# First column block of a decoder trunk: earlier shift and scale, low halves on two engines, earlier row scaling, filler products

## The chip, the core and the metric

The kernel runs on one core of a Trainium2 chip. A core has a matrix engine (TensorE, in the profile PE, its weight loads PEld), a vector engine (VectorE, DVE), an engine for activation functions (ScalarE, ACT), a general one (GpSimd, POOL) and a queue that issues transfers (SyncE, SP). Each runs its own instructions in order and waits for the others by semaphores. The metric is the device time of one execution in microseconds (us); less is better.

## What is computed

One layer of a hybrid decoder on a sequence of 2048 positions by 1024 channels, in float32. The part that matters here is its beginning:

```python
c_act = jax.nn.silu(c)
mod = c_act @ w_ada + b_ada
sh1, sc1, gt1, sh2, sc2, gt2 = jnp.split(mod, 6, axis=-1)
h = rms_norm(x, g_mix) * (1.0 + sc1) + sh1
p = h @ w_in            # columns for attention, mLSTM and spatial gating
...
x = x + gt1 * (y @ w_out)
h = rms_norm(x, g_ffn) * (1.0 + sc2) + sh2
x = x + gt2 * conv_ffn(h)
```

A shift and a scale of 1024 values each come from a vector times a matrix; every row of x is divided by its root mean square; scale and shift are applied by channel; then h goes through the input projection.

## The kernel before

**Arithmetic.** Products are exact to about float32 by splitting each operand into a rounded high half and the low half that is left (`hh` and `hl` of the activations, `wh` and `wl` of the weights). One product of two tiles is three matmuls: high by high, high by low, low by high (`mm3`, lines 54 to 56).

**Shift and scale.** `w_ada` is read in tiles of 128 rows by 512 columns, eight tiles (k = 0 to 7) for each group of 512 columns. Groups 0 and 1 give the shift, groups 2 and 3 the scale; 0 and 2 belong to channels 0 to 511, the first column block, 1 and 3 to channels 512 to 1023, the second. Tile 0 of a group goes to TensorE by itself (`column_sum(n, ada[n][0], cs)`): four products with a moving operand of one column, which the profile shows as eight instructions. Tiles 1 to 7 are multiplied by their column of `cs` and added up on DVE (`part`, lines 1116 and 1118), and the sum goes to TensorE as one more column sum (`column_sum(n, macc[n], ones)`). `first_columns` (lines 501 to 503) turns the sums of one column block into `sh1` and `a1`, with three small DVE instructions.

**First block.** Everything around the change is in `first_block` (lines 1082 to 1273). Its order is written out by hand: inside `tc.manual_schedule()` each engine runs its instructions exactly as the program lists them, through the first six of the fourteen steps of the input projection; most of what comes later is ordered by a planner. The block handles rows 0 to 511 (`x0`, four tiles of 128 rows) and then rows 512 to 1023 (`x1`, four tiles). For each tile of rows: squares with a sum on ACT (`squares`), the moments (`moments`: two small DVE instructions and a power on POOL at line 128), and a scaling by that root (`scale0` on ACT for `x0`, `scale` on DVE at line 1127 for `x1`). TensorE transposes the tiles (`turn_part`, line 611) into eight column tiles k = 0 to 7, each 128 channels by 512 rows.

`make_part(tb, k, ps)` takes one transposed tile from PSUM: ACT applies scale and shift (line 602), the high half is made on DVE or, with `on_scalar`, on ACT (line 603), and the low half on DVE (line 606). The argument `between` lets `part` steps of the next column block run on DVE between the high and the low half. `prod(t, tt, k)` multiplies 128 rows of that tile by the weights of the first projection block, 272 columns wide: three matmuls. `cur.cast()` makes the halves of those weights, the high one on ACT (line 647), the low one on POOL (line 648). The 16 gate columns of the weights are copied in by POOL (line 1159).

So the order was: sums of the first column block; eight weight casts; `part(1, 1)`; `first_columns(0)`; tiles k = 0 to 3 of the first 512 rows, with the `part(1, k)` steps between; their products; then sums of the second column block; the squares of two tiles of `x1`; `first_columns(1)`; tiles 4 to 7 and their products; the other squares; scaling of all of `x1` on DVE; its transpositions; `finish(0)`, which copies the results out and adds the gate biases (lines 1226 and 1227); and the same products for the second 512 rows.

**Loads** are all issued on SP's queue in program order: `x0`, the first and third group of `w_ada`, the block's weights, the second and fourth group, the three gate biases (lines 1091 to 1093, each spread to 128 partitions), `x1`, the weights of the next block (`nx`), small rows.

Of the kernel before, what the change touches and what calls it, by code (L numbers as in the profile page):

```python
# [8 lines left out]
F32 = mybir.dt.float32  # L9
# [8 lines left out]
P = 128  # L18
# [15 lines left out]
def trunk(  # L34
# [443 lines left out]
    def load_rest():  # L478
        r = pool.tile([P, P], F32, name="rows", tag="kw")
        dma(r[0:8], g_ffn[0].rearrange("(k p) -> k p", p=P))  # L480
        for i, g in enumerate((g_q, g_k)):
            for j in range(2):
                dma(r[8 + i : 9 + i, 64 * j : 64 * j + 64], g)
        dma(r[10:14], b_s[0])
        dma(r[14:16], g_m_out[0].rearrange("(k p) -> k p", p=P))
        return r
# [82 lines left out]

    def squares(parts):  # L570
        st = pool.tile([P, 2], F32, name="st", tag="st")
        for q, t in enumerate(parts):
            jk = pool.tile([P, 512], F32, name="jk", tag="sq")
            A.activation(jk, t, AF.Square, accum_out=st[:, q : q + 1])
        return st

    def moments(st):
        V.tensor_tensor(st[:, 0:1], st[:, 0:1], st[:, 1:2], op=ALU.add)
        V.tensor_scalar(st[:, 0:1], st[:, 0:1], 1.0 / D, EPS, op0=ALU.mult, op1=ALU.add)
        rsqrt(st[:, 0:1], 1)  # L580

    def halves(xt):
        return xt[:, 0:512], xt[:, 512:1024]
# [13 lines left out]

    def make_part(tb, k, ps, on_scalar=False, between=()):
        h32 = pool.tile([P, TB], F32, name="h32", tag="t2k")
        hh = pool.tile([P, TB], F32R, name="hh", tag="hT")  # L600
        hl = pool.tile([P, TB], F32R, name="hl", tag="hT")
        A.activation(h32, ps, AF.Identity, bias=sh1[:, k : k + 1], scale=a1[:, k : k + 1])
        (A.copy if on_scalar else V.tensor_copy)(hh, h32)
        for f in between:
            f()
        V.tensor_tensor(hl, h32, hh.bitcast(F32), op=ALU.subtract)  # L606
        hT[tb, k] = (hh, hl)

    def turn_part(ps, xs, k, i):
# [472 lines left out]
    def first_block():  # L1082
# [6 lines left out]
        for n in (1, 3):  # L1089
            ada[n] = list(load_ada(n * 512, "hT"))  # L1090
        dma(gbias[:, 0:8], b_fox_f.broadcast_to([P, 8]))
        dma(gbias[:, 8:12], b_m_i.broadcast_to([P, 4]))
        dma(gbias[:, 12:16], b_m_f.broadcast_to([P, 4]))
        x1 = []
# [11 lines left out]
        for k in range(KT):  # L1106
            nx.load()
        r16 = load_rest()
        dma(gsgu, g_sgu.broadcast_to([P, 256]))
# [15 lines left out]

        def scale(x, st):
            V.tensor_scalar(x, x, st[:, 0:1], None, op0=ALU.mult)

        def scale0(i):
            A.activation(x0[i], x0[i], AF.Copy, scale=st[i][:, 0:1])  # L1130
            turns0(i)

        st = [squares(halves(t)) for t in x0[:2]]
        moments(st[0])
        moments(st[1])
        scale0(0)
        st.append(squares(halves(x0[2])))
# [15 lines left out]
        column_sum(0, macc[0], ones[:, 0:1])  # L1153
        for k in range(4, 8):
            part(2, k)
        column_sum(2, macc[2], ones[:, 0:1])

        for k in range(KT):
            G.tensor_copy(cur.raw[k][:, 256:272], gw[:, k, :])
        for _ in range(KT):  # L1160
            cur.cast()
        part(1, 1)
        first_columns(0)
        ps = [pp.tile([P, 512], F32, name="acc", tag="acc2"), mps()]
# [11 lines left out]

        pair = lambda k: [lambda k=k: part(1, k), lambda k=k: part(1, k + 1)]
        make_part(0, 0, tp[0], True, pair(2))
# [4 lines left out]
        make_part(0, 1, tp[1], True, pair(4))  # L1183
        prod(0, 0, 1)
        prod(0, 1, 1)
        make_part(0, 2, tp[2], True, pair(6))
        tp.append(turns(x0, 5))
        prod(0, 0, 2)
        prod(0, 1, 2)
        make_part(0, 3, tp[3], True)  # L1190
        prod(0, 0, 3)
        prod(0, 1, 3)
        n_acc[0] += 1
# [5 lines left out]
        column_sum(1, macc[1], ones[:, 0:1])  # L1199
        for k in range(1, 8):  # L1200
            part(3, k)
        column_sum(3, macc[3], ones[:, 0:1])
        st = [squares(t) for t in x1[:2]]
        for t in st:
            moments(t)
        first_columns(1)
        for k in (4, 5):
            make_part(0, k, tp[k])
            tp.append(turns(x0, k + 2))
        st.append(squares(x1[2]))  # L1210
        moments(st[2])
        for tt in range(4):
            prod(0, tt, 4)
        for k in (6, 7):
            make_part(0, k, tp[k])
            for tt in range(4):
                prod(0, tt, k - 1)
        for tt in range(4):
            prod(0, tt, 7)
        st.append(squares(x1[3]))  # L1220
        moments(st[3])

        def finish(t0):
# [8 lines left out]

        for i in range(4):
            for t in x1[i]:
                scale(t, st[i])
        tps = [tr_ps(), tr_ps()]
        for i in range(4):
            for k in range(2):
                turn_part(tps[k], x1, k, i)
        finish(0)  # L1240
# [836 lines left out]
```

## Time and profile before

| | us |
|---|---|
| median of 3 runs | 2570.06 |
| lowest, highest | 2568.8, 2570.49 |
| span of the profiled execution, first to last instruction | 2567.7 |
| share of the span in which PE is busy | 98% |
| first group's products of column tiles 0 to 3 | 31.39 to 40.22 |
| shift and scale of the second column block taken up on DVE | 42.99 |
| first group's products of column tiles 4 to 7 | 46.27 to 54.07 |
| second group's first product | 56.33 |

The profile records one execution. Its page shows the span; the runs' median is 2.4 us above it, the rest lying before the first and after the last instruction. A line of a timeline gives the start, the time taken, the engine, the line of the kernel, the operation, the tile written and the tiles read with their shapes, how many instructions were merged, and in brackets how long the engine had been idle and what it was waiting for. In a view of groups the numbers after the bar are the busy time, the mean of one instruction in ns, and the idle time ahead. The granted clock of TensorE is 1.00 at full speed. Matmul ends in the trace are modelled and overlap the next start, so the step from one start to the next is what a matmul costs.

### The profile page before, as it was taken

Reading aid. Unit: us, or ns where it says so; the run is one execution under the profiler, and the core shown is the slowest. Engines: PE = TensorE matmul, PEld = TensorE weight load, DVE = VectorE, ACT = ScalarE, POOL = GpSimd, SP = SyncE. Lnnn points to the kernel's source line nnn. Section 1 sums busy time; section 2 is a strip of 40 time slices with the busy share of each in tenths; the row PEclk is TensorE's granted clock in tenths of the full one; section 3 lists DMA queues with packets and bytes.
Section 4 is the critical chain, followed back from the end, with each engine's and each line's share of the span. In section 5 each row is a group of like instructions: output and inputs, shape, how many; then the busy total and the mean of one; then the engine's idle time right before and its main releaser. Section 6 shows DMA issues by size and latency. Waiting matters only on the chain.

```text
span 2567.7 us, 36386 instructions
## 1 busy us (share of the span) xinstructions
PE 2522.9 (98%) x12553; PEld 2097.9 (82%) x12569; DVE 1993.5 (78%) x3406; ACT 1281.9 (50%) x2443; POOL 405.2 (16%) x537
## 2 busy tenths in 40 slices
PE   6999999999999999999999999999999999999999
PEld 6888888888787877778878888888888888888887
DVE  7657666576388889965689888888888888998897
ACT  5433343433388878844455444444444444444443
POOL 2013310133266557610000000000000000000000
PEclk9999999999999999999999999999999999999999
DMA  7345753455554446256823222265222218567523
GB/s 262 112 124 168 218 180 94 133 160 148 175 160 127 128 126 170 70 185 234 287 82 99 91 82 83 84 218 174 88 77 84 89 66 299 180 236 260 165 78 119
DMA packets 302672, 379.58 MB, mean 148 GB/s; under 512 B 31758, under 2 KB 194412, under 8 KB 300440
## 3 DMA queue, kind: packets, MB, share of 16 engines
q1 hardware_dynamic: 302488, 377.26, 46.6%
q8 instruction: 99, 1.62, 0.3%
q14 instruction: 85, 0.70, 0.1%
HBM read 276.44 MB, written 100.74 MB: 147 GB/s over the span
## 4 chain that ended last, share of the span: by engine, by line
PE 56%; DVE 5%; DMA 3%; ACT 2%; issue 2%; POOL 0%; SPq 0%; ACTq 0%; DVEq 0%
PE ub L55 10%; PE ub L56 10%; PE ub L54 10%; PE db L55 5%; PE db L56 5%; PE db L54 5%; PE tp L259 2%; PE sp L206 2%; PE wps L54 1%; PE op L245 1%; PE wps L55 1%; PE wps L56 1%; PE op L246 1%; ACT L L223 1%; DMA wd<-in_w_down_dram 1%
## 5 line engine op out<-in xcount | busy, mean ns | idle before, releaser
L54 PE MATMUL acc<-wh,hh 128*128 128x512 f32 (+2 forms) x752 | 280.4, 374 | 1.2 <-DVE vhl L815 1.2
L54 PE MATMUL ub<-T,wsph 128*128 128x512 f32 x704 | 273.9, 389 | 1.2 <-ACT wsph L1533 1.2
L55 PE MATMUL ub<-T,wsph 128*128 128x512 f32 x704 | 274.3, 390 | 0.2 <-DVE T L1481 0.2
L56 PE MATMUL ub<-T,wspl 128*128 128x512 f32 x704 | 273.9, 389 | 0.0
L55 PE MATMUL acc<-wl,hh 128*128 128x512 f32 (+2 forms) x752 | 269.1, 359 | 0.6 <-DVE wl L648 0.6
L56 PE MATMUL acc<-wh,hl 128*128 128x512 f32 (+2 forms) x752 | 269.5, 360 | 0.2 <-DVE hl L606 0.2
L55 PE MATMUL db<-wspl,wsph 128*128 128x512 f32 x616 | 239.7, 389 | 0.2 <-DVE wspl L1677 0.2
L54 PE MATMUL db<-wsph 128*128 128x512 f32 x616 | 239.5, 389 | 0.0
L56 PE MATMUL db<-wsph,wspl 128*128 128x512 f32 x616 | 239.5, 389 | 0.0
L1533 ACT CAST wsph<-S 128x512 fp32r<-128x512 f32 x176 | 109.3, 623 | 217.4 <-PE ub L55 152.2
L1676 ACT CAST wsph<-act 128x512 fp32r<-128x512 f32 x154 | 96.1, 624 | 231.1 <-PE db L55 220.2
L263 DVE TENSOR_TENSOR plo<-tp,phi 128x512 fp32r<-128x512 f32 (+1 forms) x320 | 186.9, 607 | 30.0 <-ACT phi L262 28.0
L55 PE MATMUL ub<-B,wsph 128*128 128x512 f32 x528 | 205.6, 389 | 1.0 <-DVE B L1481 0.9
L54 PE MATMUL ub<-B,wsph 128*128 128x512 f32 x528 | 205.7, 390 | 0.0
L56 PE MATMUL ub<-B,wspl 128*128 128x512 f32 x528 | 205.5, 389 | 0.0
L223 ACT ACTIVATE L<-L,nm 128x1024 f32<-128x1024 f32 (+2 forms) x192 | 172.6, 903 | 35.8 <-DVE nm L212 33.9
L262 ACT CAST phi<-tp 128x512 fp32r<-128x512 f32 (+1 forms) x320 | 160.2, 520 | 40.9 <-PE tp L259 39.7
L259 PE MATMUL tp<-ident,L 128*128 128x128 f32 x1088 | 176.7, 274 | 2.4 <-DVE plo L263 0.7
L206 PE MATMUL sp<-kk,q 128*128 128x512 f32 (+3 forms) x640 | 169.6, 375 | 4.0 <-DVE nm L212 3.0
L228 POOL TENSOR_SCALAR L<-L,rs 128x1024 f32<-128x1024 f32 (+2 forms) x192 | 168.0, 885 | 11.0
L56 PEld LDWEIGHTS acc<-wh,hl 128*128 128x128 f32 x752 | 142.3, 190 | 21.7 <-DVE hl L606 0.4
L55 PEld LDWEIGHTS acc<-wl,hh 128*128 128x128 f32 x752 | 143.0, 190 | 20.0 <-DVE wl L648 1.5
(336 smaller groups left out, 5943.5 us busy)
## 6 DMA issues: line engine op xcount, KB each, us to landing
w<-in_w_up_dram SPq DMA_DIRECT2D x88, 512.0 KB
wd<-in_w_down_dram SPq DMA_DIRECT2D x154, 256.0 KB
wa<-in_w_ada_dram SPq DMA_DIRECT2D x96, 256.0 KB
act_d<-yc SPq DMA_DIRECT2D x44, 512.0 KB
act<-act_d SPq DMA_DIRECT2D x44, 512.0 KB
wr<-in_w_in_dram SPq DMA_DIRECT2D x64, 256.0 KB
q<-q_d SPq DMA_DIRECT2D x128, 128.0 KB
hc_d<-hl SPq DMA_DIRECT2D x28, 512.0 KB
```

The source lines that it names most:

```text
L54: T.matmul(ps, lh, rh, start=start, stop=False, skip_group_check=resume)
L55: T.matmul(ps, lh, rl, start=False, stop=False, skip_group_check=resume)
L56: T.matmul(ps, ll, rh, start=False, stop=stop, skip_group_check=resume)
L206: T.matmul(sp[:, b : b + bw], q2[n][:, qs], kk[:, s0 + b : s0 + b + bw], start=n == 0, stop=n == 1 and not last)
L223: A.activation(L[c], L[c], AF.Exp, bias=nm[:, n - 1 : n], scale=-1.0, accum_out=rs[:, c : c + 1])
L228: G.tensor_scalar(t, t, rs[:, 0:1], 1.0, op0=ALU.mult, op1=ALU.mult)
L245: T.matmul(op[:, c0:], vv[:, j, :], hi[:, c0:], start=(j == 0), stop=False)
L259: T.transpose(tp[:, i * P : (i + 1) * P], rows[i][j // 8][:, (j % 8) * P : (j % 8 + 1) * P], ident)
L262: A.copy(hi[:, c0:], tp[:, c0:])
L263: V.tensor_tensor(lo[:, c0:], tp[:, c0:], hi[:, c0:].bitcast(F32), op=ALU.subtract)
L1533: A.copy(self.wa[p][0], self.source(p))
L1676: A.copy(hi, v)
```

## The change

- *Shift and scale of the first column block.* The eighth tile of group 2 goes to TensorE by itself, and `first_columns(0)` is called at once, ahead of the casts and of the second block's sums. The same is done with the eighth tile of group 3.
- *Sums of the second column block.* The `part` steps of groups 1 and 3 follow the first tile's low half in one run, instead of standing between the halves.
- *Low halves on two engines.* That of tile 0 stays on DVE, those of tiles 1 to 3 go to POOL. Five weight casts come ahead of tile 0, three behind it.
- *Rows of `x1`.* Tiles 0 and 1 are scaled by POOL, 2 and 3 by DVE, each as soon as its moments are there, in the middle of the first group's products; the squares of tile 2 move from ACT to DVE; the transpositions are split in two, around the last products.
- *Filler products.* `warm(n)` issues n bfloat16 products of 128 by 512 columns into a PSUM tile that nothing reads, at five places: 9, 3, 6, 8 and 5.
- *Gate biases.* Their loads move behind those of `x1` and of the next block's weights.

```diff
+    def squares(parts, on_vector=False):
...
+            if on_vector:
+                V.tensor_tensor_reduce(
+                    out=jk, in0=t, in1=t, scale=1.0, scalar=0.0, op0=ALU.mult, op1=ALU.add, accum_out=st[:, q : q + 1]
+                )
+                continue
...
+    def part_high(tb, k, ps, on_scalar=False):
...
+        return h32
+
+    def part_low(tb, k, h32, eng=V):
+        hh, hl = hT[tb, k]
+        eng.tensor_tensor(hl, h32, hh.bitcast(F32), op=ALU.subtract)
+
+    def make_part(tb, k, ps, on_scalar=False):
+        part_low(tb, k, part_high(tb, k, ps, on_scalar))
...
         nx = Weights(blocks[1][0], V, ("wr",) * 4 + ("q2k",) * 2 + ("qhl",) * 2)
         for k in range(KT):
             nx.load()
+        dma(gbias[:, 0:8], b_fox_f.broadcast_to([P, 8]))
+        dma(gbias[:, 8:12], b_m_i.broadcast_to([P, 4]))
+        dma(gbias[:, 12:16], b_m_f.broadcast_to([P, 4]))
...
+        def warm(n):
+            for _ in range(n):
+                T.matmul(misc_ps(), identb, maskT.rearrange("p h t -> p (h t)"), start=True, stop=True)
+
         st = [squares(halves(t)) for t in x0[:2]]
         moments(st[0])
         moments(st[1])
+        warm(9)
         scale0(0)
...
-        for k in range(4, 8):
+        for k in range(4, 7):
             part(2, k)
+        warm(3)
+        column_sum(2, ada[2][7], cs[:, 7:8])
         column_sum(2, macc[2], ones[:, 0:1])
+        first_columns(0)
...
-        for _ in range(KT):
+        for _ in range(5):
             cur.cast()
-        part(1, 1)
-        first_columns(0)
+        warm(6)
...
+        make_part(0, 0, tp[0], True)
+        cur.eng = G
+        for _ in range(3):
+            cur.cast()
+        for k in range(1, 8):
+            part(1, k)
+        for k in range(1, 7):
+            part(3, k)
         tp.append(turns(x0, 4))
         column_sum(1, ada[1][0], cs[:, 0:1])
         prod(0, 0, 0)
         prod(0, 1, 0)
+        for k in range(1, 4):
+            part_low(0, k, part_high(0, k, tp[k], True), G)
+            if k == 2:
+                tp.append(turns(x0, 5))
+            prod(0, 0, k)
+            prod(0, 1, k)
...
         column_sum(3, ada[3][0], cs[:, 0:1])
         column_sum(1, macc[1], ones[:, 0:1])
-        for k in range(1, 8):
-            part(3, k)
+        warm(8)
+        column_sum(3, ada[3][7], cs[:, 7:8])
         column_sum(3, macc[3], ones[:, 0:1])
-        st = [squares(t) for t in x1[:2]]
-        for t in st:
-            moments(t)
         first_columns(1)
+        warm(5)
+        st = [squares(x1[0])]
+        moments(st[0])
+        for t in x1[0]:
+            scale(t, st[0], G)
         for k in (4, 5):
             make_part(0, k, tp[k])
             tp.append(turns(x0, k + 2))
-        st.append(squares(x1[2]))
-        moments(st[2])
+        st.append(squares(x1[1]))
+        st.append(squares(x1[2], True))
         for tt in range(4):
             prod(0, tt, 4)
         for k in (6, 7):
             make_part(0, k, tp[k])
             for tt in range(4):
                 prod(0, tt, k - 1)
+            if k == 6:
+                moments(st[1])
+                for t in x1[1]:
+                    scale(t, st[1], G)
+        st.append(squares(x1[3]))
+        moments(st[2])
+        tps = [tr_ps(), tr_ps()]
+        for i in range(2):
+            for k in range(2):
+                turn_part(tps[k], x1, k, i)
+        for t in x1[2]:
+            scale(t, st[2])
         for tt in range(4):
             prod(0, tt, 7)
-        st.append(squares(x1[3]))
         moments(st[3])
+        for t in x1[3]:
+            scale(t, st[3])
+        for i in range(2, 4):
+            for k in range(2):
+                turn_part(tps[k], x1, k, i)
...
-        for i in range(4):
-            for t in x1[i]:
-                scale(t, st[i])
-        tps = [tr_ps(), tr_ps()]
-        for i in range(4):
-            for k in range(2):
-                turn_part(tps[k], x1, k, i)
         finish(0)
```

More of the change, by code (lines that the diff above doesn't have):

```diff
@@ L568, in small_setup @@
             after(4 + 2 * i, lambda i=i, r=r: turn(i, r))
-    def squares(parts):
+    def squares(parts, on_vector=False):
         st = pool.tile([P, 2], F32, name="st", tag="st")
@@ L596, in trunk @@
     hT = {}
-    def make_part(tb, k, ps, on_scalar=False, between=()):
+    def part_high(tb, k, ps, on_scalar=False):
         h32 = pool.tile([P, TB], F32, name="h32", tag="t2k")
@@ L603, in make_part @@
         (A.copy if on_scalar else V.tensor_copy)(hh, h32)
-        for f in between:
-            f()
-        V.tensor_tensor(hl, h32, hh.bitcast(F32), op=ALU.subtract)
         hT[tb, k] = (hh, hl)
+        return h32
[4 more added lines that the diff above has]
+        part_low(tb, k, part_high(tb, k, ps, on_scalar))
     def turn_part(ps, xs, k, i):
@@ L1090, in first_block @@
             ada[n] = list(load_ada(n * 512, "hT"))
-        dma(gbias[:, 0:8], b_fox_f.broadcast_to([P, 8]))
-        dma(gbias[:, 8:12], b_m_i.broadcast_to([P, 4]))
-        dma(gbias[:, 12:16], b_m_f.broadcast_to([P, 4]))
         x1 = []
@@ L1124, in turns0, with scale @@
                 turn_part(tp[k], x0, k, i)
-        def scale(x, st):
-            V.tensor_scalar(x, x, st[:, 0:1], None, op0=ALU.mult)
+        def scale(x, st, eng=V):
+            if eng is G:
+                G.tensor_scalar(x, x, st[:, 0:1], 1.0, op0=ALU.mult, op1=ALU.mult)
+            else:
+                V.tensor_scalar(x, x, st[:, 0:1], None, op0=ALU.mult)
         def scale0(i):
@@ L1175, in turns @@
             return t
-        pair = lambda k: [lambda k=k: part(1, k), lambda k=k: part(1, k + 1)]
-        make_part(0, 0, tp[0], True, pair(2))
+        make_part(0, 0, tp[0], True)
[6 more added lines that the diff above has]
+            part(3, k)
         tp.append(turns(x0, 4))
@@ L1182, in first_block @@
         prod(0, 1, 0)
[L1183 to L1192, printed above, removed]
+        for k in range(1, 4):
[4 more added lines that the diff above has]
+            prod(0, 1, k)
         n_acc[0] += 1
```

## The prediction, made before the changed kernel was run

> **What bounds the kernel now.** I read the page's head first, then the windows of the first 60 us, then the timelines of TensorE (PE), VectorE (DVE), ScalarE (ACT) and GpSimd (POOL) there; the edit touches nothing later.
>
> ```profile
> span 2567.7 us, 36386 instructions
> PE 2522.9 (98%) x12553; PEld 2097.9 (82%) x12569; DVE 1993.5 (78%) x3406; ACT 1281.9 (50%) x2443; POOL 405.2 (16%) x537
> 31.40:36.20 4.80, 4.80 (x22) 4.80 (x23) 4.69 (x9) 2.05 (x4) 0.00 (x0) 1.00 0.91 315
> 36.20:40.20 4.00, 4.00 (x33) 4.00 (x32) 3.82 (x6) 1.22 (x4) 0.00 (x0) 1.00 0.92 336
> 43.50:44.60 1.10, 0.00 (x0) 0.00 (x0) 0.00 (x0) 0.78 (x2) 0.00 (x0) 0.50 0.84 236
> 44.60:50.00 5.40, 5.35 (x24) 5.35 (x25) 5.08 (x14) 4.45 (x11) 1.09 (x2) 0.50 0.87 246
> 60.00:70.00 10.00, 10.00 (x84) 10.00 (x83) 5.32 (x9) 6.58 (x11) 0.00 (x0) 1.00 0.00 0
> ```
>
> A window's columns are its ends, its length, the busy time (and count) of PE, PEld, DVE, ACT, POOL, then granted clock, DMA share and GB/s. PE is busy 98% of the span and 10.00 of 10 us from 60 on, where the code is the same in both kernels. So I take a shift of the moment at which the second group of 512 rows starts its products to reach the end one for one. Everything is decided before that. The clock column is not enough here: 22 PE instructions in 4.80 us against 33 in 4.00 is a halved rate that the column, still at 1.00, does not record in the first 43 us. From 43.5 it does: 0.50 until 50.
>
> Now the chain of the first block.
>
> ```profile
> 18.07 4.69 DVE L1118 SCALAR_TENSOR_TENSOR modacc<-wa,cs,modacc 128x512 f32<-128x512 f32 x6
> 19.04 1.85 PE L494 MATMUL mps<-ones,modacc 128*128 128x1 f32 x8
> 22.81 1.87 PE L494 MATMUL mps<-ones,modacc 128*128 128x1 f32 x8 [1.93 <-DVE modacc L1118]
> 26.47 0.89 DVE L1116 TENSOR_SCALAR modacc<-wa,cs 128x512 f32<-128x512 f32 x1 [3.71 <-DMA wa<-in_w_ada_dram]
> 27.28 0.15 DVE L501 TENSOR_TENSOR sh<-mps,colA 128x4 f32<-128x4 f32 x1
> 34.43 1.29 DVE L606 TENSOR_TENSOR hl<-h,hh 128x512 fp32r<-128x512 f32 x2
> 40.22 0.95 PE L494 MATMUL mps<-cs,wa 128*128 128x1 f32 x8
> 41.02 1.93 PE L494 MATMUL mps<-ones,modacc 128*128 128x1 f32 x16
> 42.99 0.16 DVE L501 TENSOR_TENSOR sh<-mps,colA 128x4 f32<-128x4 f32 x1 [0.87 <-PE mps L494]
> 43.82 1.45 ACT L602 ACTIVATE h<-trp,sh,a 128x512 f32<-128x512 f32 x2 [2.15 <-DVE a L503]
> 46.16 0.69 DVE L606 TENSOR_TENSOR hl<-h,hh 128x512 fp32r<-128x512 f32 x1
> 56.33 0.39 PE L54 MATMUL acc<-wh,hh 128*128 128x272 f32 x1
> ```
>
> Four marks follow. (1) The sums of the first column block end at 22.81 + 1.87 = 24.7, but DVE takes them up at 27.28: it stands in order behind a partial sum whose DMA lands at 26.5. (2) The sixteen products of tiles k = 0 to 3 end at 40.2. (3) Three column sums (2.7 us) end at 42.95; call this moment T. Shift and scale follow, and the fifth tile starts on ACT 0.87 later. (4) The second group's products start at 56.33, which is T + 13.4.
>
> **The change part by part.** Prices:
>
> ```profile
> 5.28 0.42 DVE L448 CAST maskT<-maskf 128x512 bf16<-128x512 f32 x1
> 9.92 0.48 PE L611 MATMUL trp<-ident,xt 128*128 128x128 f32 x1 [7.27 <-ACT xt L1130]
> 28.90 0.62 ACT L603 CAST hh<-h 128x512 fp32r<-128x512 f32 x1
> 36.45 0.29 PE L54 MATMUL acc<-wh,hh 128*128 128x272 f32 x1
> 40.09 0.28 PE L56 MATMUL acc<-wh,hl 128*128 128x272 f32 x1
> 71.88 0.39 PE L55 MATMUL acc<-hl,wh 128*128 128x512 f32 x1
> 72.10 0.39 PE L56 MATMUL acc<-hh,wl 128*128 128x512 f32 x1
> L132 POOL TENSOR_TENSOR wo0l<-ld,wo0h 128x512 fp32r<-128x512 f32 x4 | 5.2, 1304 | 6.6 <-ACT wo0h L131 6.6
> L648 POOL TENSOR_TENSOR wl<-wr,wh x8: 746/752/1209, 23.5 to 28.7; 128x272 fp32r<-128x272 f32 x8
> 27.94 1.92 POOL L648 TENSOR_TENSOR wl<-wr,wh 128x272 fp32r<-128x272 f32 x2
> 27.92 2.50 DVE L1118 SCALAR_TENSOR_TENSOR modacc<-wa,cs,modacc 128x512 f32<-128x512 f32 x2
> L212 DVE CUSTOM_DVE_ANT_0 L<-sp,nf,nm 128x512 f32<-128x512 f32 x8 | 5.9, 743 | 0.0
> L228 POOL TENSOR_SCALAR L<-L,rs 128x512 f32<-128x512 f32 x16 | 11.1, 693 | 0.8
> L128 POOL TENSOR_TENSOR st<-st,nhalf 128x1 f32<-128x1 f32 x32 | 21.0, 660 | 262.2 <-DVE st L1437 152.0 <-ACT jk L574 39.6 <-DVE st L579 25.6
> ```
>
> A 272-column product is 0.22 us from start to start at the slow rate (22 in 4.80, four of them transpositions) and 0.126 at the full one (29 steps from 36.45 to 40.09). A filler has 512 columns; its own form, in bf16, is not in this stretch, so I take the 512-column product: 0.22 full (71.88 to 72.10), 0.4 slow by the same ratio. A column sum is 8 instructions: 0.95 full, 1.87 slow.
>
> First nine fillers: 9 x 0.4 = 3.6 us from the mask at 5.28 + 0.42 = 5.7, over by 9.3. The transposition that they stand ahead of starts at 9.92, when ACT's scaling lets it; that wait hides them. Without it they would cost what passes 9.92, and there is slack of 0.6.
>
> Shift and scale ahead. DVE no longer waits for the DMA of 26.5. But TensorE now has, behind the sum at 19.04 + 1.85 = 20.9, three fillers (1.2), the eighth tile's own sum (1.87) and the last sum (1.87): 25.8 at the slow rate, where the vector part is ready at 22.0 (one step of 0.78 before 18.07 + 4.69). So this comes 1.5 ahead of 27.28, not the full 2.6.
>
> Low halves on two engines. ACT casts five weight tiles, makes tile 0 (from 25.8 + 0.87 = 26.7, scale 0.73 and high half 0.62, to 28.1), then casts the other three (first ready at 28.6). POOL then has three weight halves (0.80 on average with the long one) and the low halves of tiles 1 to 3 at 1.30, where DVE took 0.69: 2.4 + 3.9 = 6.3, so 34.9 if alone. It is not alone: DVE runs thirteen partial sums beside it. In the only place where both did this, two POOL halves took 1.92 instead of 1.50 (x 1.29) and two DVE sums 2.50 instead of 1.53; the longest POOL half was 1.21 against 0.75 (x 1.6). Bounds: 34.9 and 28.6 + 6.3 x 1.6 = 38.7. At x 1.29 it is 36.7; some of DVE's work there has one SBUF input and six of the eight halves kept 0.75, so I take 36. Before, the last low half came at 34.43 + 1.29 = 35.7.
>
> On this bound the Trainium skill speaks against the change: the GPSIMD Engine Reference (section Key points) has POOL share its SBUF interfaces with VectorE, with contention when a VectorE instruction has two SBUF inputs. The trace agrees in the 1.92 and 2.50 above.
>
> TensorE after it: the third product waits for the last low half, then 4 + 24 products at 0.126 = 3.5: 39.5 instead of 40.2. The six fillers lie ahead of data that isn't there; they cost nothing.
>
> Second column block. Before, three sums, 2.7. Now four sums (3.8) and eight fillers (1.8) stand in TensorE's queue: 5.6, so T = 45.1, **2.15 later than 42.95**. DVE's share is not what is late: 13 sums at 0.78 from 28.6, slowed over the 7 us beside POOL, end near 41.
>
> From T on (offsets from T). DVE queues: shift and scale, tiles 4 and 5 with low halves until 3.9 (46.16 + 0.69 - 42.95, as before), **then two squares with sum at 0.74 in place of ACT's** (5.4), tile 6 (1.07, 6.45), the moments of row block 1 (0.33, 6.8), tile 7. POOL: root 0.66, scaling of block 1, 2 x 0.69 (8.9), root of block 2 (9.5). DVE: scaling of block 2, 0.84 (10.4), moments 0.33, POOL root 0.66 (11.4), scaling of block 3, 0.84 (12.3). TensorE: last two transpositions 0.3, ACT 0.73, high half or next transpositions 0.6, and 0.1 to 0.2 of handing over: first product at T + 14.1. The products of tiles 4 to 7 (4 x 12 x 0.126 = 6.0) fit underneath, at half clock only just. So scaling sooner buys nothing: its chain of moments, root, scale, taken block by block over two engines, ends later than before's, where four scalings ran in a row:
>
> ```profile
> 49.59 1.67 DVE L1127 TENSOR_SCALAR xt<-xt,st 128x512 f32<-128x512 f32 x4
> 51.18 1.67 DVE L1127 TENSOR_SCALAR xh<-xh,st 128x512 f32<-128x512 f32 x4
> 31.26 0.33 SPq L1091 DMA_DIRECT2D gbias<-in_b_fox_f_dram  x1
> 35.50:36.00 0.50, 0.50 (x4) 0.50 (x3) 0.50 (x2) 0.00 (x0) 0.00 (x0) 1.00 0.18 40
> 38.98 0.63 ACT L574 ACTIVATE jk<-xt 128x512 f32<-128x512 f32 x1 [5.47 <-DMA xt<-in_x_dram]
> 48.97 0.29 SPq L480 DMA_DIRECT2D rows<-in_g_ffn_dram  x1
> 53.54 0.17 DVE L1227 TENSOR_TENSOR gates<-acc,gbias 128x16 f32<-128x16 f32 x1 [0.69 <-ACT ev L1226]
> ```
>
> Three bias loads move on SP's queue from 31.26 past the next rows and the sixteen weight loads, to about where 48.97 is issued. The dip to 40 GB/s goes, and the next rows land some 1.5 earlier than 38.98; ACT then waits for T instead, so no gain. Their reader, at 53.54 now and past 56 then, leaves seven us for landing.
>
> Sum: 45.1 + 14.1 = 59.2 against 56.33, **+2.9 us**. On the profiled span 2567.7 that is 2570.6; the runs' median 2570.06 holds 2.4 us around the span, so 2573.0.
>
> **Rivals.** *The two engines block each other, or the fillers fail.* At x 1.6 the last low half is at 38.7, T at 38.7 + 3.5 + 5.6 = 47.8, products at 61.9: +5.6, 2575.7. It decides from 38.2 on, where the shift passes 5.1. The same price has a clock that falls all the same between the sums: two sums at 1.87 (+1.8) and some 0.8 on the products, +5.5. For it: 1.21 and 2.50 above, and the fall at 43 after 2.7 us of column sums, which shows that TensorE being busy with those is not enough. Against it: POOL kept 0.75 for six of eight halves, mostly while DVE was idle though. 0.25.
>
> *The fillers hold the full clock from the first.* Then the sums at 20 cost 0.95, shift and scale come at 23.5, POOL ends its weight halves at 29.8 and the low halves at 33.7, T = 33.7 + 3.5 + 5.6 = 42.8, products at 56.9: +0.6, 2570.7. Against it: the slow rate lasted to 36.4 although PE was busy from 28.9, and to 50.0 from 44.6, so only dense products raise it. 0.20. By the Trainium skill (TensorE: Matmul & The Clock Gate, What's actually happening) one busy window of some 3.4 us lifts the clock; nine fillers would do it here. The trace's 7.5 and 5.4 us agree only if sums and transpositions are not counted.
>
> *Faster.* With T = 42.8 and scaling fully hidden, TensorE's own work from T (2.9 to the first product, 6.0, two sets of transpositions 1.2, ACT and high half 1.4) gives 54.3: -2.0, 2568.0. More than 0.2% (5.1 us, about what a measurement of this kernel tells from no change) would take a gain that this profile has no place for, in the later, planned part: 0.07. That the change does nothing at all is not possible, its instructions stand in hand-written order.
>
> **How the numbers follow.** Forecast 0.48 (2571 to 2575.2), clock held 0.20, slower 0.25, faster 0.07. Within 0.2%: 0.48 + 0.20 = 0.68. Low end: the best case 2568.0 less 0.5 for the spread of runs; high end: 2575.7 with half clock behind T as well (+0.8) and 1.0 for the other bound of the squares and roots, 2577.5.
>
> **What would show it.** Shift and scale on DVE near 26 (clock held: 23.5). Low halves on POOL at 1.3 alone or 1.7 to 2.1 contended, the last at 36. T near 45 with eight fillers inside the last 5.6 us. DVE scaling of the last row block about T + 12; the second group's first product at 59. I am wrong if POOL's low halves stay under 1.3 and T lies before 43, if the clock column falls to 0.50 after 40, or if the stretch behind 60 differs in length.

## The result and the profile after

| | before | after |
|---|---|---|
| median of 8 runs each, us | 2570.65 | 2578.22 |
| lowest, highest, us | 2568.8, 2573.64 | 2575.72, 2581.48 |
| ratio, 95% interval | 1 | 1.0031 [1.0022, 1.0039] |
| span of the profiled execution, us | 2567.7 | 2577.6 |

The kernel became slower by 8 us (5.7 to 10), outside the forecast range by 0.7 us at its upper end. From here on a ratio is turned into microseconds by 2570, so 0.001 is 2.6 us.

The head of the page of the kernel after:

```profile
span 2577.6 us, 36495 instructions
PE 2542.7 (99%) x12616; PEld 2106.1 (82%) x12616; DVE 1993.4 (77%) x3401; ACT 1281.5 (50%) x2439; POOL 413.9 (16%) x544
```

TensorE is busy 19.8 us more (2542.7 against 2522.9) and the span is 9.9 longer: fillers count as busy time, so this row alone says nothing about useful work. The timeline of VectorE and GpSimd of the kernel after, with the rows that answer to the marks of the prediction:

```profile
25.88 0.16 DVE L501 TENSOR_TENSOR sh<-mps,colA 128x4 f32<-128x4 f32 x1 [3.89 <-PE mps L494]
29.51 8.16 DVE L1128 SCALAR_TENSOR_TENSOR modacc<-wa,cs,modacc 128x512 f32<-128x512 f32 x6
31.23 5.10 POOL L614 TENSOR_TENSOR hl<-h,hh 128x512 fp32r<-128x512 f32 x3
49.75 0.16 DVE L501 TENSOR_TENSOR sh<-mps,colA 128x4 f32<-128x4 f32 x1 [7.74 <-PE mps L494]
61.16 0.88 DVE L1140 TENSOR_SCALAR xh<-xh,st 128x512 f32<-128x512 f32 x2 [0.66 <-POOL st L128]
```

The first shift and scale come at 25.88 (before: 27.28), the low halves end at 31.23 + 5.10 = 36.33. Up to there nothing is lost. Then VectorE idles 7.74 us and takes the second shift and scale at 49.75, where before had 42.99: **6.8 us late**. What TensorE did in that gap (from 40.25 on; the five rows ahead, and the first two windows, are for later), in its timeline, its weight-load queue (PEld) and the windows of the same stretch:

```profile
5.76 5.73 PE L1148 MATMUL mp<-maskT,identb 128*128 128x512 bf16 x9 [2.98 <-ACT jk L579]
11.28 0.42 PE L621 MATMUL trp<-ident,xt 128*128 128x128 f32 x1
...
12.70 0.95 PE L494 MATMUL mps<-cs,wa 128*128 128x1 f32 x8
...
16.06 0.48 PE L621 MATMUL trp<-ident,xt 128*128 128x128 f32 x1 [0.94 <-ACT xt L1143]
...
17.33 1.87 PE L494 MATMUL mps<-cs,wa 128*128 128x1 f32 x8
...
40.25 0.95 PE L494 MATMUL mps<-cs,wa 128*128 128x1 f32 x8
41.06 1.03 PE L494 MATMUL mps<-ones,modacc 128*128 128x1 f32 x8
41.95 4.55 PE L1148 MATMUL mp<-maskT,identb 128*128 128x512 bf16 x8
46.30 1.70 PE L494 MATMUL mps<-cs,wa 128*128 128x1 f32 x8
47.86 1.84 PE L494 MATMUL mps<-ones,modacc 128*128 128x1 f32 x8
...
63.56 0.39 PE L54 MATMUL acc<-wh,hh 128*128 128x272 f32 x1
...
78.78 0.50 PE L54 MATMUL acc<-hh,wh 128*128 128x512 f32 x1 [0.19 <-DVE gates L1267]
```

```profile
42.82 0.10 PEld L1148 LDWEIGHTS <-identb 128*128 128x128 bf16 x1 [0.34 <-issue]
...
44.00 0.10 PEld L1148 LDWEIGHTS <-identb 128*128 128x128 bf16 x1 [0.54 <-issue]
44.64 0.10 PEld L1148 LDWEIGHTS <-identb 128*128 128x128 bf16 x1 [0.54 <-issue]
```

```profile
13.00:16.00 3.00, 1.31 (x10) 0.98 (x10) 2.48 (x5) 2.56 (x4) 0.99 (x1) 0.94 1.01 371
16.00:18.00 2.00, 1.94 (x9) 1.56 (x9) 1.94 (x4) 0.01 (x1) 0.00 (x0) 0.50 1.05 394
...
40.25:41.95 1.70, 1.70 (x18) 1.70 (x17) 1.63 (x3) 0.00 (x0) 0.00 (x0) 1.00 1.04 338
41.95:43.00 1.05, 0.94 (x5) 0.29 (x5) 0.06 (x1) 0.00 (x0) 0.00 (x0) 0.98 0.95 286
43.00:46.30 3.30, 3.02 (x6) 0.71 (x5) 0.00 (x0) 0.00 (x0) 0.00 (x0) 0.50 0.95 266
46.30:49.70 3.40, 3.40 (x18) 3.37 (x17) 0.00 (x0) 0.00 (x0) 0.00 (x0) 0.50 0.32 77
```

Two sums of 0.85 us at full clock, then eight fillers that take 46.30 - 41.95 = 4.35 us, then two sums that take 3.40 because the clock fell to 0.50 at 43, inside the fillers that were to hold it. The fillers start 0.43 us apart at full clock (42.39 to 42.82 in the weight loads) and 0.64 at half (44.00 to 44.64). The order of the built program says why. For each TensorE instruction it lists the semaphores that it waits for:

```
L1148 LDWEIGHTS identb
L1148 MATMUL mp<-maskT,identb 128x512 [waits PE_49]
L1148 LDWEIGHTS identb
L1148 MATMUL mp<-maskT,identb 128x512 [waits PE_49]
```

`misc_ps()` gives a new tile of a pool that has one buffer, so every filler must wait until the one before it has ended: TensorE waits for its own semaphore between any two fillers.

The second group's first product is at 63.56 (before 56.33: +7.23), the next block's first product at 78.78 (before 71.54: +7.24). The medians differ by 7.6. So the loss is whole by 63.6 us, and it reaches the end one for one. The remaining 2.7 us of the two profiled spans come later, in single executions: in the profile after, the clock falls to half twice more, from 374.1 to 377.4 and from 677.9 to 681.2, where the profile before stays at 1.00.

The profile shows one execution only. The mean granted clock of the eight timed runs lies between 0.992, which is the profiled run, and 0.999. Four of the runs have 0.999, which leaves at most 7.7 us of recorded half clock in a span of 2577, where this profile has 13.6 from 43 to 56.6 alone. Those four still take 2575.72 to 2578.24 us. So how long the clock was down differs from run to run, and most of the loss does not hang on it.

### The profile page after: what moved, and what is told of

It is laid out like the page before. It is cut to its first block, busy times and chain, and to the rows that moved or that the text cites. A ratio compares the mean times of both kernels' runs of the same rounds, so it can differ in the third digit from the quotient of the medians.

```text
span 2577.6 us, 36495 instructions
## 1 busy us (share of the span) xinstructions
PE 2542.7 (99%) x12616; PEld 2106.1 (82%) x12616; DVE 1993.4 (77%) x3401; ACT 1281.5 (50%) x2439; POOL 413.9 (16%) x544
## 4 chain that ended last, share of the span: by engine, by line
PE 47%; DVE 2%; DMA 1%; ACT 1%; issue 0%; SPq 0%; POOL 0%; ACTq 0%; DVEq 0%
PE ub L56 10%; PE ub L55 10%; PE ub L54 10%; PE db L56 5%; PE db L54 5%; PE db L55 5%; DMA hc_d<-hl 1%; DMA x_d<-x 0%; DVE T L1514 0%; DVE B L1514 0%; DVE hz L1505 0%; DVE wspl L1570 0%; ACT hz L1484 0%; ACT T L1510 0%; ACT yg L1463 0%
## 5 line engine op out<-in xcount | busy, mean ns | idle before, releaser
L262 ACT CAST phi<-tp 128x512 fp32r<-128x512 f32 (+1 forms) x320 | 160.2, 520 | 40.9 <-PE tp L259 39.5
```

The costliest lines, as they stand in the source:

```text
L262: A.copy(hi[:, c0:], tp[:, c0:])
```

## The experiments

The theory: the eight fillers cost their own time, 4.35 instead of 1.8, because each waits for the one before it, and they fail to hold the clock. Rivals: the new tail of the block costs (squares on two engines, scaling block by block, transpositions in two parts); the low halves on GpSimd slow the front down; the later, planned part differs.

Every experiment was timed in five rounds beside runs of the kernel before on the same chip. "Second shift" is the row of line 501, "products" the second group's first product after it, "next block" the first product of the next block, all from one profile each.

| kernel | second shift | products, after it | next block | ratio, 95% interval |
|---|---|---|---|---|
| before | 42.99 | 13.34 | 71.54 | 1 |
| after | 49.75 | 13.81 | 78.78 | 1.0031 [1.0022, 1.0039] |
| e1_no8 | 43.23 | 13.61 | 73.62 | 1.0017 [1.0009, 1.0026] |
| e2_nofill | 44.69 | 13.60 | 73.53 | 1.0011 [1.0002, 1.0020] |
| e3_onetile | 44.94 | 13.90 | 74.80 | 1.0019 [1.0010, 1.0028] |
| e4_before8 | 46.76 | 12.53 | 74.50 | 1.0021 [1.0012, 1.0031] |
| e5_low_dve | 43.70 | 13.60 | 72.52 | 1.0011 [1.0002, 1.0019] |
| e6_old_tail | 43.24 | 13.36 | 71.82 | 0.9996 [0.9987, 1.0005] |
| e7_ahead | 44.21 | 13.59 | 73.02 | 1.0005 [0.9996, 1.0014] |
| e8_spread | 44.55 | 11.21 | 70.98 | 0.9994 [0.9985, 1.0002] |
| e9_tail_alone | 42.73 | 13.60 | 71.54 | 1.0003 [0.9994, 1.0011] |
| e10_fill_old_tail | 49.85 | 12.41 | 77.47 | 1.0022 [1.0013, 1.0031] |
| e11_spread_front | 43.86 | 11.19 | 70.28 | 1.0002 [0.9993, 1.0011] |
| e12_spread_fill | 42.78 | 11.20 | 69.19 | 0.9994 [0.9986, 1.0003] |

A straight line through the thirteen changed kernels, shift of the next block against gain or loss of time, has a slope of 1.03 and leaves 1.3 us of scatter, well within the intervals (about 2.3 us to either side). So the first 70 to 80 us are enough to account for the time of all of them; no cost in the planned part is needed to explain any.

**Without the eight fillers, and without any.**

```diff
-        warm(8)
```

> The changed kernel without the eight fillers ahead of the second column block's last sums. Theory A (each filler waits for the one before it to end, 0.43 us at the full clock and 0.64 at half, so eight of them put 4.35 us into TensorE's queue and let the clock fall, which makes the two sums behind them 3.35 instead of 1.9): the second shift and scale come at about 44 instead of 49.7, the second group's products at about 57.9 instead of 63.6, and the time falls by 5 to 6 us, to about 2572.5. Theory B (the low halves on POOL and the row scaling taken block by block set the end; fillers only fill gaps): products stay near 63 and the time within 1 us of the changed kernel's 2578.

The second shift moves from 49.75 to 43.23, the next block from 78.78 to 73.62, and the kernel from 1.0031 to 1.0017. So the eight cost 5.2 us by the profiles and 3.6 of the 8 by the medians, where 5 to 6 were expected; a difference of two such ratios is uncertain by some 3 us. The kernel without any filler leaves out `warm` at all five places:

> The changed kernel without any fillers, all else as changed. Theory A: also the three and six fillers of the first column block cost what lies ahead of the first shift and scale (1.7 us, 25.9 becomes 24.3), so about 1 us more than without the eight alone, 2571 to 2572; what is left above the kernel before, 0 to 2 us, is the low halves on POOL and the scaling. Theory B: 2577 to 2578.

All fillers together cost 5.1 us (1.0031 to 1.0011). The other four places (9, 3, 6 and 5) cost at most little: 1.5 us lie between the two kernels, less than their intervals can tell. The 1.7 us expected ahead of the first shift did not come: it is at 25.45 against 25.88, because the last tile's sum now waits 0.95 us for its transfer.

**The same fillers, not waiting for each other.** All products of one call go into one tile, so nothing between them has to be released:

```diff
         def warm(n):
+            ps = misc_ps()
             for _ in range(n):
-                T.matmul(misc_ps(), identb, ...
+                T.matmul(ps, identb, ...
```

> The changed kernel with the fillers of one call all written into one PSUM tile, so that none waits for the one before. Theory A: a filler costs 0.22 us at the full clock as the forecast had it, the eight 1.8 us, the second shift and scale at about 45 and the time near 2573; if dense fillers also hold the clock, the clock column shows no 0.50 between 42 and 50. Theory B: unchanged, 2578. If the time stays although each filler costs 0.22, the waiting was not the cause.

TensorE's timeline of this kernel, its windows and its VectorE:

```profile
41.34 1.89 PE L1149 MATMUL mp<-maskT,identb 128*128 128x512 bf16 x8
43.06 0.95 PE L494 MATMUL mps<-cs,wa 128*128 128x1 f32 x8
43.87 1.03 PE L494 MATMUL mps<-ones,modacc 128*128 128x1 f32 x8
...
56.89 0.44 PE L621 MATMUL trp<-ident,xh 128*128 128x128 f32 x2 [1.34 <-DVE xh L1140]
...
58.84 0.58 PE L54 MATMUL acc<-wh,hh 128*128 128x272 f32 x1
```

```profile
42.00:48.00 6.00, 5.68 (x38) 3.89 (x37) 2.30 (x8) 2.52 (x6) 2.19 (x3) 1.00 0.95 284
48.00:58.00 10.00, 7.65 (x54) 6.60 (x54) 7.17 (x24) 5.06 (x14) 3.80 (x6) 1.00 0.34 88
58.00:62.00 4.00, 3.91 (x20) 3.91 (x21) 2.94 (x5) 2.01 (x4) 1.94 (x4) 0.57 0.29 82
```

```profile
54.55 0.88 DVE L1140 TENSOR_SCALAR xh<-xh,st 128x512 f32<-128x512 f32 x2 [1.52 <-POOL st L128]
...
56.35 0.88 DVE L1140 TENSOR_SCALAR xh<-xh,st 128x512 f32<-128x512 f32 x2 [0.66 <-POOL st L128]
```

Now eight fillers take 43.06 - 41.34 = 1.72, that is 0.215 each, the price of the prediction; the clock stays at 1.00 until 58, the last two sums take 1.7 instead of 3.4, and the second shift is at 44.94 where the prediction had 45.1. That settles the price of a filler and its cause. It doesn't make the kernel fast: the eight still stand in the queue ahead of the sums, and the products start 13.90 us after the second shift, no sooner than at half clock. The rows of VectorE show what sets this: the scaling of the last row blocks waits for GpSimd's root (1.52, then 0.66), and TensorE waits 1.34 for that scaling. With the new tail a faster TensorE finds nothing to do.

The last window shows one more loss. The clock falls at 58.15 for 3.4 us, and in the profile of e1 at 57.87, while the second group's products run. From the first of these products to the next block e3 takes 15.96 us and e1 16.78, where every other kernel takes 15.2.

**The eight fillers alone, in the kernel before,** ahead of its last column sum:

```diff
+        for _ in range(8):
+            T.matmul(misc_ps(), identb, maskT.rearrange("p h t -> p (h t)"), start=True, stop=True)
         column_sum(3, macc[3], ones[:, 0:1])
```

> The kernel before with eight fillers, each waiting for the one before, ahead of its last column sum and nothing else changed. Theory A: second shift and scale 3.5 to 5 us later than 42.99, and the time 3.5 to 5 us above the kernel before, 2574 to 2575.5. Theory B: under 1 us.

```profile
42.52 3.41 PE L1203 MATMUL mp<-maskT,identb 128*128 128x512 bf16 x8
45.77 0.95 PE L494 MATMUL mps<-ones,modacc 128*128 128x1 f32 x8
```

They take 45.77 - 42.52 = 3.25 us, 0.41 each, and the kernel loses 5.4 us (3.1 to 8.0); its second shift is 3.8 us later, as expected. Here the clock was still full for the sum behind them and fell only later (0.83 in the mean from 46.7 to 50). So waiting fillers do not always lose the clock while they run. Their own time they cost always.

**Low halves on VectorE again,** without fillers, so that it stands against the kernel without any:

```diff
-            part_low(0, k, part_high(0, k, tp[k], True), G)
+            h32 = part_high(0, k, tp[k], True)
+            if k < 3:
+                part(1, 2 * k + 2)
+                part(1, 2 * k + 3)
+            part_low(0, k, h32)
```

> No fillers, and the low halves of tiles 1 to 3 back on DVE with the second block's sums between them, all else as changed (so against the run without fillers, 2.8 to 3.2 us above the kernel before). If POOL's three halves (5.1 us beside DVE's sums, which take 1.36 instead of 0.78 there) hold the products of tiles 0 to 3, the last low half comes at 33 to 34 instead of 36.3 and the time falls by 1.5 to 2.5 us. If the row scaling is what is left, it stays within 0.7 us.

Both are at 1.0011. In the profile the last low half ends at 35.2, not at 33 to 34, and the second shift comes 1.0 us sooner than without fillers alone (43.70 against 44.69), which the medians do not show. GpSimd's three low halves take 1.70 us each, but they cost the kernel nothing that these runs can tell.

**The change without its tail, and its tail alone.** First the new front without fillers, with the old tail (squares on ACT, four scalings in a row on VectorE, transpositions behind the last products):

```diff
-        first_columns(1)
-        st = [squares(x1[0])]
-        moments(st[0])
-        for t in x1[0]:
-            scale(t, st[0], G)
+        st = [squares(t) for t in x1[:2]]
+        for t in st:
+            moments(t)
+        first_columns(1)
...
+        for i in range(4):
+            for t in x1[i]:
+                scale(t, st[i])
```

> No fillers, low halves on POOL as changed, but all that follows the second shift and scale as in the kernel before: squares on ACT, all four row blocks scaled in a row on DVE, transpositions behind the last products. If the block-by-block scaling over two engines costs what the forecast had (products at T + 14.1 instead of T + 13.4), the time falls by 0.5 to 1 us; if scaling sooner helped, it rises by up to 2 us; if the low halves are the whole of the rest, it stays.

0.9996 [0.9987, 1.0005], against 1.0011 with the new tail on the same front. Then the front of before with only the new tail, from `first_columns(1)` on the lines of the change:

```diff
-        st = [squares(t) for t in x1[:2]]
-        for t in st:
-            moments(t)
         first_columns(1)
+        st = [squares(x1[0])]
+        moments(st[0])
+        for t in x1[0]:
+            scale(t, st[0], G)
...
```

> The front of the kernel before, and only the new tail: squares on both engines, scalings block by block on GpSimd and VectorE, the transpositions placed around the last products, no fillers. Theory that the tail itself costs (two kernels with it and without fillers stood at 1.0011 of the kernel before, the one with the old tail at 0.9996): 1.0010, about +2.5 us. Rival that the tail costs nothing and that those differences came from the other order of the front: 1.0000 with an interval that holds 1. In the profile the stretch from the second shift and scale to the next block's first product: 28.5 to 29 us by both.

1.0003 [0.9994, 1.0011], and the next block starts at 71.54 in both: nearer to the rival, though the 1.0010 of the theory lies within the interval. Then the whole change with all its fillers, and the tail put back by the same edit as in e6:

> The whole change except its tail: all fillers as they are, the tail of the kernel before. If the fillers (+4.5 us, the kernel after against the kernel without any filler) and the tail (+2.8) add up: 2.8 us under the kernel after, 1.0019 of the kernel before, and the second shift and scale as late as in the kernel after, 49 to 50. If the tail costs nothing: 1.0030, as the kernel after. If the fillers do harm only together with the new tail: 1.0005 or less.

1.0022 [1.0013, 1.0031]: the fillers' damage is there without the new tail (second shift at 49.85), but 2.3 us less is lost. Three pairs thus give the tail 0.8 us (e9 against before), 2.3 (after against e10) and 3.9 (e2 against e6), each uncertain by some 3 us. The profiles say what it depends on. From the second shift to the products, the new tail takes 13.6 to 13.9 us in all six kernels that have it, whatever the clock. The old one takes 13.3 to 13.6 where the clock is at half for 6.8 us behind the second shift (before, e6, e7), 12.4 and 12.5 where it is at half for 3.4 to 3.8 (e4, e10), and 11.2 where it stays up (below). So by the profiles the new tail costs some 0.3 us at half clock, and up to 2.7 at full. For the 3.9 of the third pair that isn't enough; there the next block starts at 73.53 against 71.82, of which 1.45 lies ahead of the second shift, in the same code. Starts vary by that much from one execution to the next.

**First shift and scale ahead, alone.** In the kernel before, `first_columns(0)` stands ahead of `part(1, 1)`, the eighth tile of group 3 goes to TensorE as a sum of its own, and the bias loads come last:

```diff
-        part(1, 1)
         first_columns(0)
+        part(1, 1)
...
-        for k in range(1, 8):
+        for k in range(1, 7):
             part(3, k)
+        column_sum(3, ada[3][7], cs[:, 7:8])
```

> The kernel before with three edits alone: shift and scale of the first column block ahead of the waiting sum, the last tile of group 3 straight to TensorE, gate biases loaded last. No fillers, DVE low halves, old scaling. By the chain of the profile (DVE stood until 27.28 for sums that ended at 24.7; thirteen sums instead of fourteen behind it) the second shift and scale come 1.5 to 2.5 us sooner: 2565.5 to 2566.5 where the kernel before has 2568. If DMA landing sets this stage, no change.

A miss: the first shift came at 24.73 and the second at 44.21, later than before's 42.99. This row of its TensorE is still a product at the slow rate (0.43 modelled, 0.23 from start to start), where before had the full rate from 36.4 on:

```profile
37.71 0.43 PE L54 MATMUL acc<-wh,hh 128*128 128x272 f32 x1
```

The products started at 28.67 instead of 31.39 and spent that lead at half rate, and the fourth column sum took another 0.9 us.

**Sums spread between products, and fillers where TensorE is idle.** Built on the kernel just told, with two of the four sums moved ahead of the products of row tiles 2 and 3, and five fillers into one tile behind `first_columns(1)`, where TensorE waits for ACT anyway:

```diff
             ps.append(acc_ps())
+            if tt == 2:
+                column_sum(3, ada[3][0], cs[:, 0:1])
+            else:
+                column_sum(1, macc[1], ones[:, 0:1])
             for k in range(4):
                 prod(0, tt, k)
-        column_sum(3, ada[3][0], cs[:, 0:1])
-        column_sum(1, macc[1], ones[:, 0:1])
...
         first_columns(1)
+        wps = misc_ps()
+        for _ in range(5):
+            T.matmul(wps, identb, maskT.rearrange("p h t -> p (h t)"), start=True, stop=True)
```

> As the last one, and two column sums put between the products of tiles 0 to 3, so that fewer of them follow each other, and five fillers in one tile behind the last sum. If the clock falls because a stretch of 3.4 us holds column sums and little else, it now stays at 1.00 between 40 and 50 and the products of tiles 4 to 7 take 6 instead of 7.8 us: another 1 to 2.5 us, 2563.5 to 2565. If the clock falls all the same, as the last one.

The clock stays at 1.00, and the products come 11.21 us after the second shift instead of 13.34. Against the kernel it is built on the gain is 2.8 us (1 to 2.5 expected). Against the kernel before it is 1.5 us, half of the least that was expected, since the kernel it is built on stood at 1.0005 and had gained nothing; the interval, 0.9985 to 1.0002, holds 1. The same on the change's front, without other fillers and with the old tail:

> The front of the change without fillers, the tail of before, two column sums placed between the products, and five fillers into one tile behind the last column sum, where TensorE waits for VectorE. Theory: the sums no longer stand in a row with half-speed products behind them, the second shift and scale comes at 43.2 as with that front alone, the clock stays up through the tail, and the next block starts at 70 to 71: 0.9985 to 0.9995. Rival, that the clock in this stretch does not reach the end: 0.9996 to 1.0005.

Again 11.19, and the next block at 70.28, but 1.0002 [0.9993, 1.0011], the rival's range: what the profile shows as 1.3 us gained does not show in the medians. With six more fillers into one tile ahead of the first products, at the change's place:

```diff
         for _ in range(5):
             cur.cast()
+        warm(6)
```

> As the run before it, with six more fillers into one tile ahead of the first products. Theory: they end before the first scaled tile is there, the clock is up from about 30 instead of 35 to 38, the 28 products end 1 to 2 us earlier: second shift and scale at 42 and 0.9980 to 0.9990. Rival: the products wait for VectorE and GpSimd, not for TensorE, so the mark stays at 43 to 43.5 and the time is that of the run before it.

Its windows and its TensorE:

```profile
42.00:48.00 6.00, 5.32 (x38) 4.28 (x39) 3.73 (x11) 4.37 (x9) 0.95 (x2) 1.00 0.79 226
48.00:58.00 10.00, 9.03 (x71) 8.51 (x70) 7.83 (x22) 6.37 (x14) 2.05 (x5) 1.00 0.33 96
```

```profile
42.60 1.24 PE L1149 MATMUL mp<-maskT,identb 128*128 128x512 bf16 x4
44.46 1.32 PE L621 MATMUL trp<-ident,xt 128*128 128x128 f32 x8 [0.62 <-ACT h L607]
...
53.98 0.39 PE L54 MATMUL acc<-wh,hh 128*128 128x272 f32 x1
```

The second shift came at 42.78, not at 42, so the six bought less than the theory had: the products were at the slow rate (0.23 from start to start) until 35.7, not until 30. The clock stays at 1.00, the fillers (one of the five is missing from the trace) are over 0.6 us before ACT's tile is there, the products start at 53.98 (before: 56.33) and the next block at 69.19, 2.35 us earlier than before's. Its median is 2567.75 against 2568.36, 0.9994 [0.9986, 1.0003]; the spread kernel on before's front has the same ratio. Both beat the kernel after clearly. That either beats the kernel before is likely by the profile, but not shown by the times: the interval of each holds 1.

## Why the prediction was wrong, step by step

**The step that failed** is the price of the fillers in the second column block. The prediction had no row of the form itself and took the 512-column product that streams without waiting: "0.22 full, 0.4 slow". One of the prediction's own signs of being wrong came with it: the clock column falls to 0.50 after 40. Two terms of the sum were too small.

- *Eight fillers, 1.8 us.* Measured 4.35. In one tile, without waits, they cost 1.72, so the price was right for a filler that waits for nothing. What the prediction overlooked stands in the program, not in the profile: `misc_ps()` inside the loop, and one buffer in the pool that it draws from (`("mp", 2048, 1)`).
- *Four sums, 3.8 us, at full clock.* Measured 1.70 + 3.40 = 5.1 in the profiled run: the clock fell at 43 in the middle of the fillers. The prediction had this as a rival ("a clock that falls all the same between the sums"), with 1.8 us for two sums, nearly what they lost (3.40 against 1.70), and the chance that it gave to the group of that rival was 0.25.

Together 9.45 instead of 5.6. With the products ending at 40.25 instead of 39.5 this makes the second shift 4.6 us later than the forecast 45.1. The forecast of +2.9 us plus 4.6 is 7.5, less 0.3 because the tail took 13.81 instead of 14.1: 7.2, as measured at the products. With the waits taken out (e3) the second shift is at 44.94 and the time at 1.0019, some 4.9 us above the kernel before.

**What held.**

- *First shift and scale:* forecast 25.8, measured 25.88. The three fillers ahead of it took 22.43 - 20.77 = 1.7 instead of 1.2.
- *Low halves on GpSimd:* forecast 36 at its last one, measured 36.33. With VectorE beside it they took 1.70 us each instead of 1.30 (x 1.31), as the factor 1.29 had it. The rival of two engines that block each other (x 1.6) did not come. The forecast also had TensorE wait for that half, and this did not come: from 16.06 to 62 TensorE is never idle, and it reached the product that reads the half only at 36.75.
- *The tail:* forecast products 14.1 after the second shift, measured 13.81, and VectorE's last scaling began 11.4 after it (forecast 11.4). That scaling sooner buys nothing agrees with the tail alone (1.0003 [0.9994, 1.0011], which would still hold a gain of 1.5 us).
- *The bias loads* at the end of SP's queue: no reader was late, and the rows of x1 arrived 1.5 us earlier, for nothing.
- *One for one to the end:* slope 1.03 over thirteen kernels.

**What held by luck.** The first nine fillers were to be over at 9.3, hidden by a wait until 9.92. TensorE's timeline of the kernel after, above, has the first transposition behind them at 11.28: 0.61 us each, not 0.4. The cover was gone by 1.4 us, and it still cost nothing, because TensorE waits for ACT again, 0.81 us ahead of the third row tile's transpositions and 0.94 ahead of the fourth's at 16.06. The six fillers at 25.70 took 3.6 us and ended at 29.3. They were not hidden: without fillers (e2) the first products start at 29.67, here at 31.70. By these profiles the 2 us did no harm: in e2 TensorE then waits 1.11 us for GpSimd's first low half and runs at the slow rate until 38.3, here until 36.1, so that its products end at 41.02 against 40.25.

**What the prediction read too narrowly.** It took from the slow rate before that "only dense products raise" the clock, against its rival that the fillers hold it from the first. The rival was half right. From 12.2 on TensorE of the kernel after runs at full rate, behind the nine fillers, which waited for each other, and four transpositions: the column sum at 12.70 takes 0.95 us, before's at 13.09 takes 1.71. But at 15.64 the clock falls again, and the sum at 17.33 takes 1.87. So fillers like these can raise the clock, and it does not last to the sums that set the first shift.

**What the forecast could not have gained.** Even a clock that holds was worth only what the tail lets through. With full clock up to 58 and the new tail (e3), products came 13.90 after the second shift; with full clock and the old tail (e8, e11, e12) 11.2. The change paid for the clock and moved the work that needed it behind a chain of moments, root and scaling on two other engines.

## What to carry to other kernels

A product that is there only to keep TensorE busy must not wait for anything, itself included: write all of them into one tile, and look for a wait on the engine's own semaphore in the order of the program before pricing it by a streaming row. Place such products where the engine would stand idle, never ahead of work that someone waits for; here five behind the last sum and six ahead of the first products, each set in one tile, cost nothing that the runs show, and eight waiting ones between the sums cost 3.6 us by the medians. And before buying a faster engine, check in the trace which engine sets the next step: with the old order of the scaling the full clock was worth 2.2 us to that step (13.4 to 11.2), with the new one nothing.

## What the runs showed of the hardware that was not expected

- A 512-column bf16 product that waits for its predecessor to end starts 0.41 to 0.43 us after it at full clock and 0.61 to 0.64 at half, against 0.215 without that wait at full clock.
- The Trainium skill (TensorE: Matmul & The Clock Gate, What's actually happening) describes the clock as gated by how busy TensorE has been in a window of about 3.4 us. The traces agree: the clock changes on a raster of 3.41 us. In the kernel after it changes at 15.64, 36.12, 42.95 and 56.60 (6, 2 and 4 times 3.41 us apart), in e1 at 16.90, 33.98, 44.22, 47.63, 57.87 and 61.28 (5, 3, 1, 3 and 1 times). Where the raster lies differs from one execution to the next: behind the same nine fillers TensorE runs at full rate from 12.2 on in the kernel after, while in e1 the transpositions from 12.20 to 12.89 are still at half rate (0.21 us apart against 0.11). This may be a part of the spread between executions of one program.
- What makes a stretch busy enough is not settled by these runs. From 43 to 46.3 the waiting fillers of the kernel after show as busy for 3.02 of 3.30 us, and the clock is at 0.50 all the while, whereas the same fillers without gaps kept 1.00 up to 58; so the gaps may count against them. But with the same waiting fillers e4 kept the full clock until 48.86, behind their end, and nine of them with four transpositions raised it. In the kernel before, which has none, it fell at 43.22, after 2.7 us of column sums.
- VectorE's partial sums beside GpSimd's low halves took 8.16 / 6 = 1.36 us each instead of 0.78, a loss of 3.5 us on VectorE that nobody waited for. The loss is larger on VectorE (x 1.75) than on GpSimd (x 1.31).
